# Time-step projection of the state-space branch: computed with the attention values, turned, and kept in DRAM

## The chip, the cores and the metric

The kernel runs on one core of one Trainium2 chip. Its time is the device time of one execution in microseconds (us); several executions are made and the median is given. Five engines work side by side, each with its own in-order queue of instructions: TensorE (PE in the profile, with its weight loads listed as PEld), VectorE (DVE), ScalarE (ACT), GpSimd (POOL) and SyncE (SP), which here only issues DMAs. Semaphores order the engines against each other. A profile is one execution recorded by the hardware; its clock starts with the first instruction, and its "span" is a little shorter than the device time of the same execution.

## The reference

One layer of a diffusion backbone over 512 latent tokens with 256 context tokens, model width 1024, float32. Cut to what matters here:

```python
p_lat = h_lat @ w_in                      # 512 x 1024 by 1024 x D_IN
p_ctx = h_ctx @ w_in                      # 256 tokens
# columns of w_in: z | x,B,C | dt (64) | q (1024) | k (256) | v (256) | gates
dt = softplus(p[..., DT0:Q0] + dt_bias)   # 2 directions x 32 heads
la = dt * (-exp(a_log))                   # log decay of each step
...                                       # chunked scans need cumulative sums of la
v_l = p_lat[..., V0:G0]                   # 4 value heads of 64
att = window_ctx_attention(q, k, v, kc, vc, sink)
out = (g_ssd * (y_ssd @ w_o_ssd) + g_att * (att @ w_o_att)) @ w_out
```

The 64 `dt` columns are the steps of the state-space branch. In the columns of `w_in` they lie apart from the 256 value columns, and nothing of the attention needs them; the state-space branch needs them before its first chunk.

## The kernel before

Every product is made in split float32: an operand x is rounded to a fast format (`hi`) and the rest x - hi is kept (`lo`), and three matmuls hi*hi, hi*lo, lo*hi are summed in PSUM. `load` (L154) fetches a weight piece of at most 128x1024 into one of three `wraw` buffers by a DMA on SP's queue, ACT rounds it to `whi` (L149), DVE subtracts to `wlo` (L150); there are two buffers each of `whi` and `wlo`. `run` (L167) loads one piece ahead of the step that uses it. The building tool then orders each engine's queue itself, by readiness and its own estimates, except where the code fixes PE's order.

The normal product `gemm` (L186) holds a 128x128 block of the weight matrix in the array and streams tokens: 512 latent columns, or 256 context columns, per matmul. Its output has channels on the partitions and tokens along the free axis. The values are made the other way round: `v_step` (L616) holds a 128-token block of the activations `hlh`/`hll` (latent) or `hch`/`hcl` (context) in the array and streams the 256 value columns of the weights, so that tokens come out on the partitions, as the attention's last product wants them. Six token blocks share three PSUM banks, two blocks of 256 columns to a bank. ACT and DVE then write `vst` as hi and lo (L633, L634).

The order of the work: modulation and norms; key, query and value steps; attention in 16 blocks (4 value heads by 4 query blocks, `block`, L650), between which query, key and `z` gate steps are set as other work for PE; then `att_split` (L834), three more `z` steps, and the attention's output projection in eight steps `oa_step` (L839). Behind the first of these stands `dt_tables` (L753): it makes the 64 `dt` columns with `gemm` (24 matmuls of 512 and 24 of 256 columns, 64 output channels, its own weight piece `wdt` of 128x512), adds the bias (L761, L762) and then works through softplus, logarithms, running sums and exponentials on ACT and DVE (L764 to L814), with small DMAs that park results in DRAM. The remaining `oa` steps keep PE at work meanwhile. `dt_turn` (L819) turns the tables by transposes on PE when the last `oa` step is through, and the state-space stage begins.

PSUM has eight banks. Up to `v_step` they are split as three `acc` and five `mis`; for the attention they are given to other pools (`psum_pools`, L648), and a new pool's bank is used once the old user of that bank has been read out.

Of the kernel before, what the change touches and what calls it, by code (L numbers as in the profile page):

```python
# [9 lines left out]
F32 = mybir.dt.float32  # L10
F32R = mybir.dt.float32r
U8 = mybir.dt.uint8
AF = mybir.ActivationFunctionType
ALU = mybir.AluOpType
# [4 lines left out]
P = 128  # L19
D = 1024  # L20
L = 512
LC = 256
KT = D // P
# [16 lines left out]
def raw(ap):  # L40
    return ap.bitcast(F32)
# [3 lines left out]
def tile_hybrid_layer(  # L45
# [11 lines left out]
    wk: bass.AP,  # L57
    wv: bass.AP,
    wq: bass.AP,
    wdt: bass.AP,  # L60
    wx: bass.AP,
    wz: bass.AP,
    wg: bass.AP,
# [13 lines left out]
    nc = tc.nc  # L77
    V, S, G, T = nc.vector, nc.scalar, nc.gpsimd, nc.tensor
# [5 lines left out]
    dpool = ctx.enter_context(tc.tile_pool(name="dpool", bufs=1, space=DRAM))  # L84
# [22 lines left out]
    def accb():  # L107
        return bank("acc")

    def misb():  # L110
        return bank("mis")
# [5 lines left out]


    src = {}
    src["dt", 0] = wdt, 512  # L120
    for i in range(2):
        src["k", i] = wk[i], 1024
        src["v", i] = wv[i], 1024
    for i in range(8):
        src["q", i] = wq[i], 1024
        src["oa", i] = woa[i], 1024
# [40 lines left out]
    def run(prog, ahead=1):  # L167
        seq = [k for keys, _ in prog for k in keys]
        have, nload, nuse = {}, 0, 0
        for keys, fn in prog:  # L170
            nuse += len(keys)
            while nload < min(nuse + ahead, len(seq)):
                have[seq[nload]] = load(seq[nload])
                nload += 1
            fn(*[have.pop(k) for k in keys])
# [10 lines left out]
    def gemm(targets, w, nk=KT, m=P, k0=0, first=True, last=True, ks=None):  # L186
        hi, lo = w
        for k in range(nk) if ks is None else ks:
            wh, wl = hi[:, k * m : (k + 1) * m], lo[:, k * m : (k + 1) * m]
            a, b = first and k == 0, last and k == nk - 1  # L190
            for ps, xh, xl in targets:
                T.matmul(ps, wh, xh[:, k0 + k, :], start=a, stop=False)  # L192
                T.matmul(ps, wh, xl[:, k0 + k, :], start=False, stop=False)  # L193
            for ps, xh, xl in targets:
                T.matmul(ps, wl, xh[:, k0 + k, :], start=False, stop=b)  # L195
            if BETWEEN and k % 3 == 1:
                BETWEEN.pop(0)()
# [21 lines left out]
    ao_d = dpool.tile([8, P, L], F32, name="ao_d")  # L219
    yz_d = dpool.tile([16, P, L], F32, name="yz_d")  # L220
    cs_d = dpool.tile([64, L], F32, name="cs_d")
    tt_d = dpool.tile([64, 4], F32, name="tt_d")

    def col(base, i):
# [72 lines left out]
    with tc.tile_pool(name="spool", bufs=1) as sp:  # L297
# [206 lines left out]
        for i in range(NG):  # L504
            t = tmp("tb")
# [109 lines left out]

    def v_step(*w):  # L616

        pos = [misb() for _ in range(3)]
        for k in range(KT):
            wh, wl = (z[:, (k % 4) * 256 : (k % 4 + 1) * 256] for z in w[k // 4])  # L620
            for p, po in enumerate(pos):
                hh, hl, c0 = (hlh, hll, 2 * p) if p < 2 else (hch, hcl, 0)
                for t in range(2):
                    c = slice((c0 + t) * P, (c0 + t + 1) * P)
                    o = po[:, t * 256 : (t + 1) * 256]
                    T.matmul(o, hh[:, k, c], wh, start=k == 0 and t == 0, stop=False, skip_group_check=True)
                    T.matmul(o, hh[:, k, c], wl, start=False, stop=False, skip_group_check=True)
                    T.matmul(o, hl[:, k, c], wh, start=False, stop=k == KT - 1, skip_group_check=True)
        for p, po in enumerate(pos):
            for t in range(2):  # L630
                o = po[:, t * 256 : (t + 1) * 256].rearrange("p (h d) -> p h d", h=4)
                v = vst[:, 2 * p + t, :, :]
                S.copy(v[:, :, 0:64], o)  # L633
                V.tensor_tensor(v[:, :, 64:128], o, raw(v[:, :, 0:64]), ALU.subtract)  # L634

    def q_step(t):
        def fn(w):
            ps = accb()
            gemm([LAT(ps)], w)
            q_split(ps, t)  # L640

        return [("q", t)], fn

    k_step(0)[1](first["w"][0])
    q_step(0)[1](first["w"][1])
    run([q_step(1), ([("v", 0), ("v", 1)], v_step)])

    psum_pools(acc=(2, 1), score=(1, 2), pt=(3, 1), po=(1, 1))  # L648

# [100 lines left out]
    atth = ep.tile([P, 8, L], F32R, name="atth")  # L750
    attl = ep.tile([P, 8, L], F32R, name="attl")

    def dt_tables(w):  # L753
        pl, pc = accb(), accb()
        gemm([(pl[:64, :L], hlh, hll), (pc[:64, :LC], hch, hcl)], w, m=64)
        shp = [64, 768]
        v = ep.tile(shp, F32, tag="d0", name="dv")
        e = ep.tile(shp, F32, tag="d1", name="de")
        u = ep.tile(shp, F32, tag="d2", name="du")
        u2 = ep.tile(shp, F32, tag="d3", name="du2")  # L760
        S.activation(v[:, :L], pl[:64, :L], AF.Identity, bias=dtv[:, 0:1])  # L761
        S.activation(v[:, L:], pc[:64, :LC], AF.Identity, bias=dtv[:, 0:1])  # L762
        nA = cpool.tile([64, 1], F32, name="nA")
        S.activation(nA, dtv[:, 1:2], AF.Exp)  # L764
        V.tensor_scalar_mul(nA, nA, -1.0)
# [81 lines left out]
        return [("oa", o)], fn  # L847

    oas = [oa_step(o) for o in range(8)]
    run([([], att_split)] + fill[n1:n2] + oas[:1] + [([("dt", 0)], dt_tables)] + oas[1:] + [([], dt_turn)])  # L850
    epool.close()
    att_pool.close()

# [588 lines left out]
def pack(  # L1442
# [31 lines left out]
    d["wm2"] = ca(w_mod[:, 2048:].reshape(4, 2, P, 8, 512).transpose(3, 0, 2, 1, 4).reshape(8, 4, P, 1024))  # L1474
    d["wq"] = _cols(w_in, perm(q0, 16))
    d["wk"] = _cols(w_in, perm(k0, 4))
    d["wv"] = ca(w_in[:, v0:g0].reshape(2, 4, P, 256).transpose(0, 2, 1, 3).reshape(2, P, 1024))
    d["w0"] = ca(w_in[:, g0 : g0 + 640].reshape(KT, P, 640))
    d["wdt"] = ca(w_in[:, dt0:q0].reshape(KT, P, 64).transpose(1, 0, 2).reshape(P, 512))
    d["wx"] = _cols(w_in, A(xbc0, dt0))  # L1480
    d["wz"] = _cols(w_in, A(z0, xbc0))
    d["wg"] = _cols(w_in, A(g0, g0 + 2048))
# [30 lines left out]
```

## Time and profile before

| | |
|---|---|
| median of 3 runs | 1293.3 us (1292.84 to 1293.32) |
| the profiled execution, its own time | 1291.25 us |
| its span | 1289.5 us |
| PE busy | 1260.1 us, 98% of the span |
| DVE / ACT / POOL busy | 899.2 / 664.8 / 138.6 us |
| DMA | 168.66 MB, mean 131 GB/s |

A line of the timeline reads: start, duration, engine, line of the code, operation, output<-inputs, shape, count, and in brackets how long the engine sat idle before it and which engine's work released it. The recorded duration of a matmul contains its way through the array, and the next one starts before it ends; what a matmul costs in a stream is the distance from its start to the next start. A row of stretches ("windows") gives, for a stretch of the span, the busy time of PE, PEld, DVE, ACT and POOL with the number of instructions in brackets, then the granted TensorE clock, the share of DMA and GB/s. A row of groups gives line, engine, operation, shape, count, busy time, mean of one in ns, and idle time ahead. A row of waits gives who waited for whom: us in total, how often, the longest.

### The profile page before, as it was taken

To read this page: it belongs to the slowest core of one execution; us is meant where nothing else is said; L and a number is where in the kernel's file an instruction comes from. 1 tells how busy PE (TensorE), PEld (TensorE's weight loads), DVE (VectorE), ACT (ScalarE), POOL (GpSimd) and SP (SyncE) were. 2 spreads that over 40 slices of the span, in tenths; PEclk is the share of its full clock that TensorE was granted. 3 is DMA by queue.
4 is the path that set the end of the run, shared out by engine and by line. 5 is a ranking of instruction groups with operands and counts; after the bars stand their busy time and mean duration, and the time that the engine had idled before them with its cause. 6 is when DMAs were issued, how large, how long until landed. Compare 5 with 4: busy or idle time off the path is not lost.

```text
span 1289.5 us, 17298 instructions
## 1 busy us (share of the span) xinstructions
PE 1260.1 (98%) x6482; PEld 1025.6 (80%) x6482; DVE 899.2 (70%) x1431; ACT 664.8 (52%) x1230; POOL 138.6 (11%) x113
## 2 busy tenths in 40 slices
PE   7999999999999999999999999999999999999997
PEld 4698777887778878788787777888888888888886
DVE  3867888778495588888888757776677767772323
ACT  3568888767434466475673744223544444442221
POOL 0000000000000043433434440000200000000000
PEclk9999999999999999999999999999999999999999
DMA  8621112222345245454445558867133433333331
GB/s 321 255 94 51 42 58 66 66 74 66 99 127 184 82 117 137 139 134 131 137 140 170 165 192 290 252 221 229 33 115 115 131 114 114 115 107 93 92 101 66
DMA packets 86931, 168.66 MB, mean 131 GB/s; under 512 B 6784, under 2 KB 42112, under 8 KB 86848
## 3 DMA queue, kind: packets, MB, share of 16 engines
q1 hardware_dynamic: 86848, 167.56, 41.5%
q8 instruction: 51, 0.84, 0.3%
q14 instruction: 32, 0.26, 0.1%
HBM read 150.62 MB, written 16.91 MB: 130 GB/s over the span
## 4 chain that ended last, share of the span: by engine, by line
PE 84%; DVE 7%; ACT 5%; issue 2%; DMA 1%; POOL 0%; SPq 0%; DVEq 0%; ACTq 0%; POOLq 0%
PE acc L193 21%; PE acc L192 21%; PE acc L195 21%; PE mis L1054 2%; PE mis L1047 2%; PE score L668 2%; PE pt L697 2%; PE mis L404 2%; PE mis L960 1%; PE po L702 1%; DVE wlo L150 1%; PE mis L888 1%; PE mis L978 1%; PE po L703 1%; PE acc L1196 1%
## 5 line engine op out<-in xcount | busy, mean ns | idle before, releaser
L150 DVE TENSOR_TENSOR wlo<-wraw,whi 128x1024 fp32r<-128x1024 f32 x161 | 203.8, 1266 | 133.0 <-ACT whi L149 131.7
L149 ACT CAST whi<-wraw 128x1024 fp32r<-128x1024 f32 x161 | 166.7, 1036 | 220.7 <-PE acc L193 186.6
L192 PE MATMUL acc<-hlh,whi 128*128 128x512 f32 (+1 forms) x496 | 204.1, 412 | 0.1
L193 PE MATMUL acc<-hll,whi 128*128 128x512 f32 (+1 forms) x496 | 196.1, 395 | 0.0
L195 PE MATMUL acc<-hlh,wlo 128*128 128x512 f32 (+1 forms) x496 | 195.4, 394 | 0.2 <-DVE wlo L150 0.2
L192 PE MATMUL acc<-mh,whi 128*128 128x512 f32 x376 | 146.5, 390 | 0.0
L193 PE MATMUL acc<-ml,whi 128*128 128x512 f32 x376 | 146.4, 389 | 0.0
L195 PE MATMUL acc<-mh,wlo 128*128 128x512 f32 x376 | 146.3, 389 | 0.0
L192 PEld LDWEIGHTS acc<-hlh,whi 128*128 128x128 f32 (+1 forms) x496 | 93.0, 187 | 21.3 <-issue 4.1
L193 PEld LDWEIGHTS acc<-hll,whi 128*128 128x128 f32 (+1 forms) x496 | 93.0, 187 | 19.9 <-issue 4.1
L195 PEld LDWEIGHTS acc<-hlh,wlo 128*128 128x128 f32 (+1 forms) x496 | 92.8, 187 | 19.5 <-issue 1.0
L195 PEld LDWEIGHTS acc<-mh,wlo 128*128 128x128 f32 x376 | 70.6, 188 | 14.8
L192 PEld LDWEIGHTS acc<-mh,whi 128*128 128x128 f32 x376 | 70.6, 188 | 14.7
L193 PEld LDWEIGHTS acc<-ml,whi 128*128 128x128 f32 x376 | 70.6, 188 | 14.6 <-DVE ml L1165 0.2
L962 POOL TENSOR_TENSOR st<-st,eT 128x512 f32<-128x512 f32 x24 | 32.8, 1368 | 410.3 <-ACT st L980 396.7
L860 ACT ACTIVATE ta<-acc,half 128x512 f32<-128x512 f32 (+1 forms) x66 | 46.6, 706 | 41.0 <-PE acc L195 41.0
L245 POOL TENSOR_TENSOR rs<-ms,phalf 128x2 f32<-128x2 f32 (+1 forms) x7 | 6.1, 877 | 548.9 <-DVE ms L244 548.9
L675 DVE CUSTOM_DVE_ANT_0 p<-score,winm,nsink 128x512 f32<-128x512 f32 (+1 forms) x64 | 52.0, 812 | 15.0 <-PE score L668 14.2
L192 PE MATMUL acc<-fh,whi 128*128 128x512 f32 x154 | 60.0, 390 | 0.0
L195 PE MATMUL acc<-fh,wlo 128*128 128x512 f32 x154 | 59.9, 389 | 0.0
L193 PE MATMUL acc<-fl,whi 128*128 128x512 f32 x154 | 59.9, 389 | 0.0
L679 ACT ACTIVATE p<-p,mneg 128x512 f32<-128x512 f32 (+1 forms) x64 | 49.7, 777 | 17.2 <-DVE mneg L675 16.9
(320 smaller groups left out, 2818.8 us busy)
## 6 DMA issues: line engine op xcount, KB each, us to landing
wraw<-wup SPq DMA_DIRECT2D x44, 512.0 KB, 3.6
fb<-cs_d SPq DMA_DIRECT2D x32, 512.0 KB, 6.7
wraw<-wm SPq DMA_DIRECT2D x32, 512.0 KB, 3.6
wraw<-wx SPq DMA_DIRECT2D x24, 512.0 KB, 3.6
wm<-wm SPq DMA_DIRECT2D x16, 512.0 KB, 8.1
wraw<-wz SPq DMA_DIRECT2D x16, 512.0 KB, 3.6
wraw<-wos SPq DMA_DIRECT2D x16, 512.0 KB, 4.6
wraw<-wdn SPq DMA_DIRECT2D x16, 512.0 KB, 3.5
```

The source lines that it names most:

```text
L149: S.copy(hi[:, :n], r[:, :n])
L150: V.tensor_tensor(lo[:, :n], r[:, :n], raw(hi[:, :n]), ALU.subtract)
L192: T.matmul(ps, wh, xh[:, k0 + k, :], start=a, stop=False)
L193: T.matmul(ps, wh, xl[:, k0 + k, :], start=False, stop=False)
L195: T.matmul(ps, wl, xh[:, k0 + k, :], start=False, stop=b)
L404: T.matmul(pg[i], w[a][:, i * P : (i + 1) * P], h[b], start=st and a + b == 0, stop=en and a == 1, skip_group_check=True,)
L668: T.matmul(ps[:, o : o + w], Q[h][:, b * P : (b + 1) * P], k[:, j, z[0] * P : z[0] * P + w], start=v == 0 and o % 512 in (0, P), stop=v == ...
L675: V.tensor_tensor_reduce(p[:, :n], ps[:, o0 : o0 + n], m, op0=ALU.add, op1=ALU.min, scale=1.0, scalar=nsink[:, h : h + 1], accum_out=mn,)
L679: S.activation(p[:, :n], p[:, :n], AF.Exp, bias=mn, scale=-1.0, accum_out=den[:, i : i + 1])
L697: T.transpose(pt[:, i * P : (i + 1) * P], pts[i][:, c * P : (c + 1) * P], ident)
L860: S.activation(o[:, :n], ps[:, :n], AF.Identity, scale=hcol(base_w, stride + i), bias=hcol(base_b, i))
L962: G.tensor_tensor(h8(n), h8(s), bc64(eT[:, z0 : z0 + 8, c]), ALU.mult)
```

## The change

The 64 step columns are joined to the 256 value columns on the host: the weight array `wv` becomes three pieces of 960, 960 and 640 columns (three, three and two blocks of 128 input rows with 320 columns each), and `wdt` goes. `v_step` now streams 320 columns per matmul, with each of the six token blocks in a PSUM bank of its own (five `mis`, one `acc`); the number of matmuls stays 144. After each block's two `vst` operations ACT copies the 64 step columns to SBUF (`steps`), PE turns the six 128x64 blocks by transposes into two banks, ACT copies these out, and two DMAs on SP's queue write them to a new DRAM array `dt_d` (64x768). `dt_tables` has no product any more: it reads `dt_d` by one DMA on SP's queue into `v` and adds the bias there in one ACT instruction.

```diff
     src = {}
-    src["dt", 0] = wdt, 512
+    for i, n in enumerate((3, 3, 2)):
+        src["v", i] = wv[i, :, : n * 320], n * 320
     for i in range(2):
         src["k", i] = wk[i], 1024
-        src["v", i] = wv[i], 1024
...
+    dt_d = dpool.tile([64, L + LC], F32, name="dt_d")
...
     def v_step(*w):
 
-        pos = [misb() for _ in range(3)]
+        pos = [misb() for _ in range(5)] + [accb()]
         for k in range(KT):
-            wh, wl = (z[:, (k % 4) * 256 : (k % 4 + 1) * 256] for z in w[k // 4])
-            for p, po in enumerate(pos):
-                hh, hl, c0 = (hlh, hll, 2 * p) if p < 2 else (hch, hcl, 0)
-                for t in range(2):
-                    c = slice((c0 + t) * P, (c0 + t + 1) * P)
-                    o = po[:, t * 256 : (t + 1) * 256]
-                    T.matmul(o, hh[:, k, c], wh, start=k == 0 and t == 0, stop=False, skip_group_check=True)
-                    T.matmul(o, hh[:, k, c], wl, start=False, stop=False, skip_group_check=True)
-                    T.matmul(o, hl[:, k, c], wh, start=False, stop=k == KT - 1, skip_group_check=True)
-        for p, po in enumerate(pos):
-            for t in range(2):
-                o = po[:, t * 256 : (t + 1) * 256].rearrange("p (h d) -> p h d", h=4)
-                v = vst[:, 2 * p + t, :, :]
-                S.copy(v[:, :, 0:64], o)
-                V.tensor_tensor(v[:, :, 64:128], o, raw(v[:, :, 0:64]), ALU.subtract)
+            wh, wl = (z[:, (k % 3) * 320 : (k % 3 + 1) * 320] for z in w[k // 3])
+            for t, po in enumerate(pos):
+                hh, hl, c0 = (hlh, hll, t) if t < 4 else (hch, hcl, t - 4)
+                c, o = slice(c0 * P, (c0 + 1) * P), po[:, 0:320]
+                T.matmul(o, hh[:, k, c], wh, start=k == 0, stop=False)
+                T.matmul(o, hh[:, k, c], wl, start=False, stop=False)
+                T.matmul(o, hl[:, k, c], wh, start=False, stop=k == KT - 1)
+        steps = tmp("te")
+        for t, po in enumerate(pos):
+            o = po[:, 0:256].rearrange("p (h d) -> p h d", h=4)
+            S.copy(vst[:, t, :, 0:64], o)
+            V.tensor_tensor(vst[:, t, :, 64:128], o, raw(vst[:, t, :, 0:64]), ALU.subtract)
+            S.copy(steps[:, t * 64 : (t + 1) * 64], po[:, 256:320])
+        for t0, t1 in ((0, 4), (4, 6)):
+            ps, n = misb(), (t1 - t0) * P
+            for t in range(t0, t1):
+                T.transpose(ps[:64, (t - t0) * P : (t - t0 + 1) * P], steps[:, t * 64 : (t + 1) * 64], ident)
+            o = tmp("tc")
+            S.copy(o[:64, :n], ps[:64, :n])
+            nc.sync.dma_start(dt_d[:, t0 * P : t1 * P], o[:64, :n])
...
-    run([q_step(1), ([("v", 0), ("v", 1)], v_step)])
+    run([q_step(1), ([("v", i) for i in range(3)], v_step)])
...
-    def dt_tables(w):
-        pl, pc = accb(), accb()
-        gemm([(pl[:64, :L], hlh, hll), (pc[:64, :LC], hch, hcl)], w, m=64)
+    def dt_tables():
         shp = [64, 768]
         v = ep.tile(shp, F32, tag="d0", name="dv")
...
-        S.activation(v[:, :L], pl[:64, :L], AF.Identity, bias=dtv[:, 0:1])
-        S.activation(v[:, L:], pc[:64, :LC], AF.Identity, bias=dtv[:, 0:1])
+        nc.sync.dma_start(v, dt_d)
+        S.activation(v, v, AF.Identity, bias=dtv[:, 0:1])
...
-    run([([], att_split)] + fill[n1:n2] + oas[:1] + [([("dt", 0)], dt_tables)] + oas[1:] + [([], dt_turn)])
+    run([([], att_split)] + fill[n1:n2] + oas[:1] + [([], dt_tables)] + oas[1:] + [([], dt_turn)])
```

More of the change, by code (lines that the diff above doesn't have):

```diff
@@ L59, in tile_hybrid_layer @@
     wq: bass.AP,
-    wdt: bass.AP,
     wx: bass.AP,
@@ L1476, in pack @@
     d["wk"] = _cols(w_in, perm(k0, 4))
-    d["wv"] = ca(w_in[:, v0:g0].reshape(2, 4, P, 256).transpose(0, 2, 1, 3).reshape(2, P, 1024))
+    vdt = ca(w_in[:, np.r_[v0:g0, dt0:q0]].reshape(KT, P, 320).transpose(1, 0, 2)).reshape(P, KT * 320)
+    d["wv"] = ca(np.pad(vdt, ((0, 0), (0, 320))).reshape(P, 3, 960).transpose(1, 0, 2))
     d["w0"] = ca(w_in[:, g0 : g0 + 640].reshape(KT, P, 640))
-    d["wdt"] = ca(w_in[:, dt0:q0].reshape(KT, P, 64).transpose(1, 0, 2).reshape(P, 512))
     d["wx"] = _cols(w_in, A(xbc0, dt0))
```

## The prediction

> **What bounds the kernel now.** I read the page first (busy shares, clock, chain), then the stretches and waits of the attention, then the timeline where the change takes something away or puts something in.
>
> ```profile
> span 1289.5 us, 17298 instructions
> PE 1260.1 (98%) x6482; PEld 1025.6 (80%) x6482; DVE 899.2 (70%) x1431; ACT 664.8 (52%) x1230; POOL 138.6 (11%) x113
> ...
> PEclk9999999999999999999999999999999999999999
> ...
> PE 84%; DVE 7%; ACT 5%; issue 2%; DMA 1%; POOL 0%; SPq 0%; DVEq 0%; ACTq 0%; POOLq 0%
> ```
>
> PE is busy throughout at full clock, and 84% of the chain that ended last is PE. So a matmul taken out is worth its distance to the next start, and anything that makes PE stand still costs its full length. Only the attention comes near another limit:
>
> ```profile
> 0.00:10.00 10.00, 3.18 (x20) 1.36 (x20) 1.22 (x8) 1.87 (x3) 0.74 (x9) 1.00 0.78 268
> ...
> 110.00:162.00 52.00, 50.90 (x280) 40.83 (x278) 46.59 (x100) 47.06 (x95) 0.00 (x0) 1.00 0.13 41
> 200.00:314.00 114.00, 113.72 (x609) 92.11 (x608) 89.79 (x191) 85.59 (x169) 0.00 (x0) 1.00 0.22 69
> ```
> ```profile
> PE pt L697 <- ACT p L688: 1.2, 1, 1.2
> PE po L702 <- ACT pth L700: 0.7, 2, 0.5
> ```
>
> From 110 to 162 us DVE (46.59) and ACT (47.06 of 52) are at 90%; from 200 on they have room. The longest wait of PE between 98.5 and 330 us is 1.2.
>
> **The product that goes.** The step columns are made between these two starts:
>
> ```profile
> 343.61 0.40 PE L192 MATMUL acc<-hlh,whi 128*64 128x512 f32 x1
> ...
> 351.90 0.40 PE L192 MATMUL acc<-atth,whi 128*128 128x512 f32 x1
> ```
>
> 351.90 - 343.61 = 8.3 us of PE without a gap: -8.3. Its split goes too, but the three new value pieces (960, 960, 640) hold as many columns as the two old ones and the step piece, so ACT and DVE have the same to round.
>
> **The wider value product.** The 144 matmuls stay and stream 320 columns instead of 256.
>
> ```profile
> 81.11 0.28 PE L626 MATMUL mis<-whi,hlh 128*128 128x256 f32 x1
> ...
> 98.29 0.28 PE L627 MATMUL mis<-wlo,hch 128*128 128x256 f32 x1
> 98.41 0.28 PE L628 MATMUL mis<-whi,hcl 128*128 128x256 f32 x1
> 98.53 0.40 PE L192 MATMUL acc<-hlh,whi 128*128 128x512 f32 x1
> ...
> 101.28 0.39 PE L192 MATMUL acc<-hlh,whi 128*128 128x512 f32 x1
> 101.51 0.39 PE L193 MATMUL acc<-hll,whi 128*128 128x512 f32 x1
> ```
>
> A start every 0.120 us at 256 columns, 0.23 at 512; on the line between them 320 columns take 0.1475. 144 x 0.0275 = +4.0, bounds 3.8 and 4.2. The second weight piece is now needed after three blocks of input rows instead of four. Its `wlo` is made here:
>
> ```profile
> 88.64 1.22 DVE L150 TENSOR_TENSOR wlo<-wraw,whi 128x1024 fp32r<-128x1024 f32 x1
> ...
> 89.96 0.34 PE L627 MATMUL mis<-wlo,hlh 128*128 128x256 f32 x1
> ```
>
> Before, PE reached it at 89.96, just as it was ready. Now it arrives at 81.11 + 54 x 0.1475 + the same 0.1 of start-up = 89.2, plus one matmul, while DVE, whose order there is the same, ends near 89.8: +0.5 (0 if DVE comes earlier, 0.7 at most). The third piece has until the sixth block: no cost.
>
> **The turn.** In the order in which the new kernel is built the six transposes stand directly behind the last value product, so PE, in order, stands until ACT has brought out all six step blocks. Before, 15 query matmuls followed there and hid ACT's copies.
>
> ```profile
> 98.01 1.37 ACT L633 CAST vst<-mis 128x256 fp32r<-128x256 f32 x4 [0.29 <-PE mis L628]
> 99.27 1.06 ACT L149 CAST whi<-wraw 128x1024 fp32r<-128x1024 f32 x1
> ...
> 98.42 1.48 DVE L634 TENSOR_TENSOR vst<-mis,vst 128x256 fp32r<-128x256 f32 x4 [0.24 <-ACT vst L633]
> ...
> 391.74 0.60 PE L827 MATMUL mis<-ident,dsb 128*128 128x128 f32 x4
> 392.27 0.33 PE L831 MATMUL mis<-ident,dsa 64*128 64x64 f32 x2
> ```
> ```profile
> L832 ACT COPY TC<-mis 128x128 f32<-128x128 f32 x1 | 0.3, 290 | 0.0
> ```
>
> Call T the moment PE could issue on. The last value matmul's record ends 0.16 after it (98.41 + 0.28 against 98.53); in the last round a block is done every 3 x 0.1475 = 0.44, so block 0 is ready at T - 2.05. ACT then has six `vst` copies (1.37/4 = 0.34), six step copies (estimate 0.25, under the 0.29 of a 128x128 copy) and, in its new order between the fourth and fifth of them, one `whi` rounding of 1.05: 2.0 + 1.5 + 1.05 = 4.6, so T + 2.55. Each step copy also waits for DVE's subtraction of its block (0.37 each, beside it): +0.2. Only the last transpose (0.13) is left then: PE goes on at T + 2.9. Ends: 1.9 if the rounding falls behind the copies, 3.7 if a step copy takes a `vst` copy's time and waits grow; I take +2.9. The turn uses the banks of blocks 0 and 1, and one of them goes to the score pool; its copy out (about 0.6 on ACT, ended by T + 3.4) is through when PE, after three query matmuls (0.7), comes to the first score at T + 3.6: 0, and up to 0.6 if the copies are late. The two writes to `dt_d` stand on SP's queue behind the four weight loads that PE needs next and ahead of two whose buffers are not free yet: 0, covered by the loads' own wait; the one value load more is paid for by the step load that goes.
>
> **The tables.** The chain of `dt_tables` starts behind `att_split` instead of behind the product, some three steps earlier. On ACT and DVE it now lies across the `z` steps:
>
> ```profile
> 329.09 1.05 ACT L149 CAST whi<-wraw 128x1024 fp32r<-128x1024 f32 x1
> 332.70 1.05 ACT L149 CAST whi<-wraw 128x1024 fp32r<-128x1024 f32 x1 [2.55 <-PE acc L193]
> ...
> 354.65 0.85 ACT L767 ACTIVATE de<-de 64x768 f32<-64x768 f32 x1
> ...
> 355.53 0.55 DVE L768 TENSOR_SCALAR du<-de 64x768 f32<-64x768 f32 x1 [1.15 <-ACT de L767]
> 356.12 4.95 DVE L769 RECIPROCAL du<-du 64x768 f32<-64x768 f32 x1
> ...
> 338.17 0.39 PE L192 MATMUL acc<-atth,whi 128*128 128x512 f32 x1
> ...
> 384.83 0.39 PE L193 MATMUL acc<-attl,whi 128*128 128x512 f32 x1
> 386.18 0.50 PE L195 MATMUL acc<-atth,wlo 128*128 128x512 f32 x1 [0.96 <-DVE wlo L150]
> ```
>
> On the old clock, and in the built order of the new kernel, ACT comes to the bias after the rounding that ends at 330.1, three instructions of 0.85 end at 332.65, DVE adds (0.55) and takes the reciprocal to 338.15. Behind it in DVE's new order stand the `z` read-out (0.6) and then the `wlo` of the first output step (1.2): ready at 339.9. PE starts that step at 338.17 and wants `wlo` two matmuls later, 338.62: +1.3 (0 if the chain is late enough to let the split ahead, 2 at most). The later splits lead their use by 3 us or more, but the one behind the running sums just arrives. The old stall at 384.83 (1.35 from start to start instead of 0.23: 1.1) goes with the chain's earlier end: -1.1. The read of `dt_d` waits on SP for PE, at the latest for the attention's last product:
>
> ```profile
> 323.35 0.43 PE L703 MATMUL po<-ptl,vst 128*128 128x512 f32 x1
> ```
> ```profile
> fb<-cs_d SPq DMA_DIRECT2D x32, 512.0 KB, 6.7
> ...
> ts_d<-tb SPq DMA_DIRECT2D x8, 256.0 KB, 2.1
> ```
>
> From 323.8 it lands after 2.1 to 6.7, at 325.9 to 330.5; ACT wants it at 330.1. I take 0 (the 192 KB lie nearer the 256 KB row), at most 0.4. [...]
>
> **The sum** on the profiled execution: -8.3 + 4.0 + 0.5 + 2.9 + 1.3 - 1.1 = -0.7. Then the attention, whose first score was here:
>
> ```profile
> 101.96 0.28 PE L668 MATMUL score<-khi,q 128*128 128x256 f32 x1
> ```
>
> It moves to 98.5 + 4.0 + 0.5 + 3.6 = 106.6, 4.6 later, while PE is 7.4 behind (4.0 + 0.5 + 2.9): only 3 query matmuls stand ahead of the first score in the built order, where 15 stood, so 12 x 0.227 = 2.7 us of covering work move into the stretch where ACT and DVE are at 90%. What they fill there is regained, 0 to 2.7; PE's recorded idle time from 110 to 162 is 52 - 50.9 = 1.1, starts lie late also without idle time, so I take the half, -1.3. In all -2.0: 1289.2 for the execution that took 1291.25. That execution lies 2.05 under the median of 1293.3; taken off the median: 1291.3. About 0.2%, 2.6 us, is what a measurement of this kernel can tell from no change, and -2.0 lies inside.
>
> **Rivals.** *The attention is bound by ACT and DVE (faster).* For it: the 90%. Against: PE hardly idles. All 2.7 come back and the first output step's split slips ahead of the reciprocal: -0.7 - 2.7 - 1.3 = -4.7, 1288.6.
>
> *The transposes of the attention lose their cover (slower).* In the new order of PE the first block's transposes stand 26 projection matmuls behind the first score instead of 32, the fourth block's 93 instead of 105. If softmax is not ready sooner, PE stands for what is missing, 18 x 0.227 = 4.1, and nothing is regained: -0.7 + 4.1 = +3.4, 1296.7. It decides once PE waits 3.3 us more than now at L697 and L702. Against: most other blocks have more cover than before.
>
> *The clock falls at the turn.* The turn makes the longest stand of PE inside the kernel's body. If PE ran at half its rate afterwards for as long as it stood, 2.9 us, half of that is lost: -2.0 + 1.5 = -0.5, 1292.8. Against it: in the first 10 us PE was busy for 3.18 only and the granted clock is 1.00 all the same. [...]
>
> **How the numbers follow.** Forecast as summed, its regained part between nothing and most of the 2.7: chance 0.60, of which 0.20 is faster by over 2.6. ACT and DVE as the bound: 0.20, faster. Lost cover: 0.16, slower. Clock: 0.04, half of it slower. So faster 0.40, same 0.42, slower 0.18. The forecast's own range is 1289.5 to 1292.6; with the rivals 8 in 10 lie between 1287.5 and 1295.5.
>
> **What would show it.** The value matmuls 0.1475 apart; PE standing some 2 to 3 us at the six transposes; a wait of about 1.3 for `wlo` in the first output step and none near the running sums; no 64-channel products behind the first output step. I am wrong if the turn costs 1 or 5, or if PE's waits inside the attention change by more than 3.

## The result, and the profile after

The changed kernel takes 1296.16 us (median of 7 executions, 1293.60 to 1299.63), the kernel before, run beside it on the same chip, 1292.84 (7 executions, 1291.53 to 1293.32). The ratio is 1.0029, with a 95% interval of 1.0015 to 1.0043: slower by 0.3%. Forecast was 1291.3, between 1289.5 and 1292.6; with the rivals the range ended at 1295.5, and the result lies above that too. The profiled execution of the changed kernel took 1295.57 us with a span of 1293.8; that of the kernel before 1291.25 and 1289.5. So the traces are 4.3 us apart, the medians 3.3. In the changed kernel the lines from L191 on are one lower than before in `gemm` (L194 is the product with `wlo`), and four to five higher in the attention (L673 is the score, L680 the row maximum, L702 the transposes, L707 and L708 the last products).

Where the 4.3 us come in is read from the starts of the same instructions in both timelines:

| on PE | before | after | later by |
|---|---|---|---|
| first value product | 81.11 | 81.53 | 0.42 |
| last value product | 98.41 | 102.50 | 4.09 |
| first query product behind the value step and the turn | 98.53 | 104.61 | 6.08 |
| first score | 101.96 | 105.39 | 3.43 |
| first output step | 338.17 | 348.87 | 10.70 |
| turn of the tables | 391.31 | 393.54 | 2.23 |
| first down step | 1156.40 | 1160.21 | 3.81 |
| end of the span | 1289.5 | 1293.8 | 4.3 |

From 98.53 to 338.17 the kernel before needs 239.64 us; the changed one needs 244.26 from 104.61 to 348.87: 4.6 more for the same 1243 matmuls. From the first output step to the turn of the tables it saves 8.47. The first view is the value step and the turn, on PE and then on ACT:

```profile
81.53 0.31 PE L624 MATMUL mis<-whi,hlh 128*128 128x320 f32 x1
...
102.50 0.31 PE L626 MATMUL acc<-whi,hcl 128*128 128x320 f32 x1
102.65 1.04 PE L636 MATMUL mis<-ident,te 128*64 128x128 f32 x4
104.44 0.41 PE L636 MATMUL mis<-ident,te 128*64 128x128 f32 x2 [0.76 <-ACT te L632]
104.61 0.48 PE L191 MATMUL acc<-hlh,whi 128*128 128x512 f32 x1
```
```profile
103.12 0.22 ACT L632 COPY te<-mis 128x64 f32<-128x64 f32 x1
103.22 1.06 ACT L148 CAST whi<-wraw 128x1024 fp32r<-128x1024 f32 x1
104.17 0.22 ACT L632 COPY te<-mis 128x64 f32<-128x64 f32 x1
104.27 0.23 ACT L632 COPY te<-acc 128x64 f32<-128x64 f32 x1
```

The value products start 20.97/143 = 0.147 us apart. The turn takes PE from 102.65 to 104.61, 1.96 us, with the weight rounding between the step copies. The second view is DVE's timeline around 155 us, then PE's; the third is PE's waits between 98 and 345 us.

```profile
149.97 0.75 DVE L680 CUSTOM_DVE_ANT_0 p<-score,winm,nsink 128x512 f32<-128x512 f32 x1
...
152.02 2.84 DVE L590 TENSOR_TENSOR klo<-tb,khi 64x512 fp32r<-64x512 f32 x4
155.13 1.77 DVE L590 TENSOR_TENSOR klo<-tc,khi 64x256 fp32r<-64x256 f32 x4 [0.28 <-ACT khi L589]
156.94 0.75 DVE L680 CUSTOM_DVE_ANT_0 p<-score,winm,nsink 128x512 f32<-128x512 f32 x1
```
```profile
154.70 0.39 PE L192 MATMUL acc<-hll,whi 128*128 128x512 f32 x1
157.75 0.38 PE L673 MATMUL score<-khi,q 128*128 128x256 f32 x1 [2.66 <-DVE mneg L680]
...
159.48 0.63 PE L191 MATMUL acc<-hlh,whi 128*128 128x512 f32 x1
159.91 0.63 PE L192 MATMUL acc<-hll,whi 128*128 128x512 f32 x1
```
```profile
PE score L673 <- DVE mneg L680: 3.3, 2, 2.7
PE po L707 <- ACT pth L705: 1.6, 4, 0.5
PE pt L702 <- ACT p L693: 1.3, 2, 1.2
```

All eight rests of the second key step (`klo`, 2.84 + 1.77 us) stand in DVE's queue in one lump ahead of a row maximum. The score bank is free only when that maximum has read it, so PE stands 2.66 us, the longest wait of the whole attention; the longest before was 1.2. Behind it the matmuls of 512 columns start 0.43 apart where they start 0.23 apart elsewhere. In the kernel before the same rests were spread out: the four of 512 columns stood one by one between 140.43 and 145.80, and only the four of 256 columns stood together ahead of a row maximum:

```profile
140.43 0.68 DVE L590 TENSOR_TENSOR klo<-tb,khi 64x512 fp32r<-64x512 f32 x1
...
149.22 0.75 DVE L675 CUSTOM_DVE_ANT_0 p<-score,winm,nsink 128x512 f32<-128x512 f32 x1
...
149.90 1.77 DVE L590 TENSOR_TENSOR klo<-tc,khi 64x256 fp32r<-64x256 f32 x4
151.70 0.75 DVE L675 CUSTOM_DVE_ANT_0 p<-score,winm,nsink 128x512 f32<-128x512 f32 x1
```

The fourth view is a row of stretches of the changed kernel, each 3.41 us long (the columns are those explained above; the clock is the third number from the end):

```profile
151.19:154.60 3.41, 3.41 (x18) 2.87 (x18) 3.27 (x6) 3.29 (x6) 0.00 (x0) 1.00 0.00 0
154.60:158.01 3.41, 0.75 (x5) 0.33 (x4) 3.01 (x8) 3.29 (x9) 0.00 (x0) 1.00 0.00 0
158.01:161.42 3.41, 3.30 (x12) 2.62 (x12) 3.30 (x5) 1.59 (x5) 0.00 (x0) 0.50 0.40 115
...
772.41:775.82 3.41, 1.87 (x13) 1.61 (x11) 1.48 (x3) 1.18 (x3) 1.02 (x1) 1.00 0.93 298
775.82:779.23 3.41, 3.23 (x8) 2.29 (x8) 3.41 (x6) 3.41 (x6) 0.00 (x0) 0.50 0.93 322
```

The clock is exactly halved for one stretch of 3.41 us (a cell, below) after PE was busy for only 0.75 us of the stretch before, and again at 775.82. A third such stretch lies at 28.3 us. In work that PE bounds each costs half its length, 1.7 us (an estimate from the length and the halved rate). The one at 775.82, where DVE and ACT are busy throughout, cost less: PE's lag behind the kernel before is 3.0 us at the product ahead of it and 3.6 behind it. The profiled execution of the kernel before has none inside its body, which is part of the 4.3 us between the traces; by the mean clocks of their executions (0.991 to 0.996 after; 0.991 to 0.998 before, in the sessions below) both kernels have some in most executions, the changed one about one more.

The last view is the first output step, DVE and then PE:

```profile
344.05 4.94 DVE L772 RECIPROCAL du<-du 64x768 f32<-64x768 f32 x1
...
349.46 1.20 DVE L149 TENSOR_TENSOR wlo<-wraw,whi 128x1024 fp32r<-128x1024 f32 x1
```
```profile
348.87 0.39 PE L191 MATMUL acc<-atth,whi 128*128 128x512 f32 x1
...
350.72 0.50 PE L194 MATMUL acc<-atth,wlo 128*128 128x512 f32 x1
```

`wlo` waits behind the reciprocal and the `z` read-out, as foreseen. Between 348.87 and 350.72 lie four matmuls, 0.9 us of work in 1.85: the hold-up costs 0.9. The longest wait recorded for PE there is another, 0.46 at 349.94 for a weight rounding on ACT, but it lies inside the same stretch: the product with `wlo` could not start before DVE's subtraction ended at 350.66.

### The profile page after: what moved, and what is told of

Read it like the earlier page. It is cut to its first block, busy times and chain, and to the rows that moved or that the text cites. A ratio compares the mean times of both kernels' runs of the same rounds, so it can differ in the third digit from the quotient of the medians.

```text
span 1293.8 us, 17232 instructions
## 1 busy us (share of the span) xinstructions
PE 1258.9 (97%) x6440; PEld 1027.5 (79%) x6440; DVE 899.7 (70%) x1431; ACT 666.1 (51%) x1237; POOL 138.4 (11%) x113
## 4 chain that ended last, share of the span: by engine, by line
PE 82%; ACT 7%; DVE 5%; issue 2%; DMA 2%; POOL 0%; SPq 0%; DVEq 0%; ACTq 0%; POOLq 0%
PE acc L194 20%; PE acc L191 20%; PE acc L192 20%; PE score L673 2%; PE mis L1057 2%; PE mis L1050 2%; PE pt L702 2%; PE mis L404 2%; PE mis L963 1%; PE po L707 1%; DVE wlo L149 1%; ACT whi L148 1%; PE po L708 1%; ACT ta L577 1%; PE mis L981 1%
## 5 line engine op out<-in xcount | busy, mean ns | idle before, releaser
L149 DVE TENSOR_TENSOR wlo<-wraw,whi 128x1024 fp32r<-128x1024 f32 (+1 forms) x161 | 203.9, 1267 | 136.9 <-ACT whi L148 131.5
L148 ACT CAST whi<-wraw 128x1024 fp32r<-128x1024 f32 (+1 forms) x161 | 166.6, 1035 | 220.9 <-PE acc L192 163.8
L191 PE MATMUL acc<-hlh,whi 128*128 128x512 f32 x488 | 201.7, 413 | 0.0
L194 PE MATMUL acc<-hlh,wlo 128*128 128x512 f32 x488 | 193.1, 396 | 0.5 <-DVE wlo L149 0.3
L192 PE MATMUL acc<-hll,whi 128*128 128x512 f32 x488 | 193.3, 396 | 0.0
L191 PE MATMUL acc<-mh,whi 128*128 128x512 f32 x376 | 146.6, 390 | 0.0
L194 PE MATMUL acc<-mh,wlo 128*128 128x512 f32 x376 | 146.4, 389 | 0.0
L191 PEld LDWEIGHTS acc<-hlh,whi 128*128 128x128 f32 x488 | 92.1, 189 | 20.3 <-issue 4.1
L194 PEld LDWEIGHTS acc<-hlh,wlo 128*128 128x128 f32 x488 | 92.0, 189 | 20.2 <-DVE wlo L149 1.5
L192 PEld LDWEIGHTS acc<-hll,whi 128*128 128x128 f32 x488 | 92.1, 189 | 20.0 <-issue 4.1
L194 PEld LDWEIGHTS acc<-mh,wlo 128*128 128x128 f32 x376 | 70.6, 188 | 14.8
L191 PEld LDWEIGHTS acc<-mh,whi 128*128 128x128 f32 x376 | 70.6, 188 | 14.3
L680 DVE CUSTOM_DVE_ANT_0 p<-score,winm,nsink 128x512 f32<-128x512 f32 (+1 forms) x64 | 52.0, 813 | 16.9 <-PE score L673 15.2
L191 PE MATMUL acc<-fh,whi 128*128 128x512 f32 x154 | 60.1, 390 | 0.0
L194 PE MATMUL acc<-fh,wlo 128*128 128x512 f32 x154 | 60.0, 389 | 0.0
```

The lines of the kernel that those rows point to most:

```text
L148: S.copy(hi[:, :n], r[:, :n])
L149: V.tensor_tensor(lo[:, :n], r[:, :n], raw(hi[:, :n]), ALU.subtract)
L680: V.tensor_tensor_reduce(p[:, :n], ps[:, o0 : o0 + n], m, op0=ALU.add, op1=ALU.min, scale=1.0, scalar=nsink[:, h : h + 1], accum_out=mn,)
```

## The experiments

Theory one was formed from the two traces: what makes the difference is one wait of PE behind the eight key rests, and the halved clock that follows it. Its rivals were that the attention as a whole is short of DVE and ACT, that every order of the attention has waits of its own, and, for the clock, that a stand must have a certain length. Each row of the table compares with the kernel before in the same session and on the same chip; e8, the kernel with the stands, was executed once, in 1310.14 us. Where the expectations of e1 and e2 speak of 244.3 and 239.6 us "between the first score and the first output step", they mean the stretch from the first query product; from the first score it is 243.5 and 236.2.

| run | median us | before us | ratio (95%) |
|---|---|---|---|
| e1 changed, key rests on POOL | 1292.60 | 1293.61 | 0.9991 (0.9980 to 1.0001) |
| e2 before, key rests on POOL | 1301.04 | 1293.61 | 1.0054 (1.0039 to 1.0069) |
| e3 before, key step one block earlier | 1299.86 | 1293.61 | 1.0045 (1.0030 to 1.0059) |
| e4 before, no step product | 1286.04 | 1293.61 | 0.9935 (0.9919 to 0.9951) |
| e5 changed, turn late | 1295.83 | 1293.40 | 1.0018 (1.0009 to 1.0028) |
| e6 changed, no turn | 1295.32 | 1293.40 | 1.0013 (1.0004 to 1.0022) |
| e7 changed, turn late, rests on POOL | 1291.44 | 1293.40 | 0.9986 (0.9977 to 0.9994) |
| e9 changed, raw steps kept | 1301.55 | 1293.24 | 1.0065 (1.0053 to 1.0078) |
| e10 the same, rests on POOL | 1296.29 | 1293.24 | 1.0027 (1.0016 to 1.0038) |
| e11 changed, half of the rests on POOL | 1294.55 | 1293.24 | 1.0008 (0.9998 to 1.0017) |
| e12 e10 with an early read | 1290.71 | 1293.58 | 0.9978 (0.9969 to 0.9987) |

**The key rests on POOL (e1, e2).** The edit, the same in both kernels:

```diff
-    def split_k(r, t, lo, hi):
+    def split_k(r, t, lo, hi, E=V):
...
-            for b in (0, 64):
+            for b in (a, 64 - a):
                 S.copy(khi[b : b + 64, j, lo:hi], r[a : a + 64, :n])
-                V.tensor_tensor(klo[b : b + 64, j, lo:hi], r[a : a + 64, :n], raw(khi[b : b + 64, j, lo:hi]), ALU.subtract)
+                z = a if E is G else b
+                E.tensor_tensor(klo[b : b + 64, j, lo:hi], r[a : a + 64, :n], raw(khi[z : z + 64, j, lo:hi]), ALU.subtract)
...
-            split_k(rope(pl, -0.125), t, 0, L)
+            split_k(rope(pl, -0.125), t, 0, L, G if t else V)
...
-            split_k(rc, t, L, 768)
+            split_k(rc, t, L, 768, G if t else V)
```

> The changed kernel, with the eight key rests (klo) of the second key step made on POOL instead of DVE; everything computed stays. Theory one (a single wait: the eight rests stand in DVE's queue ahead of a row maximum, PE stands 2.7 us behind it, and the clock is then halved for 3.4 us, which costs 1.7): the wait at the score matmul near 158 us goes and with it the halved clock behind it, so about 1296.2 - 2.7 - 1.7 = 1291.8, between 1291 and 1293. Rival (the attention as a whole is short of DVE and ACT or of cover for its transposes): the wait comes back at other places, the attention keeps its 244.3 us between the first score and the first output step, and the time stays between 1295 and 1297.

Measured: 1292.60, within the range and 3.6 us below the changed kernel's median; by the two ratios it is 0.0038 of 1293, or 4.9. PE's waits of the profiled execution:

```profile
PE score L674 <- DVE mneg L681: 1.8, 4, 0.7
```

The wait of 2.7 is gone, no halved clock lies between 17 and 1283 us, and PE comes to the first output step at 344.83 where it came at 348.87. Theory one holds in place and, within a microsecond, in size. What stays is 1.0 us: from its first query product behind the turn, at 104.25, the stretch takes 240.6, where the kernel before has 239.6. A second loss of about 2 us lies behind the tables: this execution is 1.8 us ahead of the kernel before at the turn of the tables (389.52 against 391.31) and 0.2 behind it at the first down step (1156.56 against 1156.40), at full clock throughout. One new wait of PE for DVE there is 1.1 (L234); the rest was not followed up. With 3.7 for the value step and 2.0 for the turn, these two losses use up the 8.5 us that the output steps save in this trace.

> The control for it: the kernel before, with the same eight key rests on POOL; everything computed stays. Theory one: the kernel before has no such wait, so taking 4.6 us of work off DVE changes little: 1292.8, between 1292 and 1294, with 239.6 us between first score and first output step. Rival (DVE bounds the attention): the kernel before gains too, 1 to 4 us, 1289 to 1292.

Measured: 1301.04, which neither expected. PE's waits, from 98 to 420 us, name the place:

```profile
PE acc L192 <- DVE te L522: 3.7, 1, 3.7
PE acc L195 <- DVE wlo L150: 2.3, 2, 1.3
```

The new built order lets a `z` read-out on DVE come late near 320 us, and two cells of halved clock follow there (321 to 328 us). Freeing DVE of 4.6 us made this order worse, so the attention isn't simply short of DVE; and moving these rests to POOL is no gain in itself. As a control it is a weak one, since the move gave the kernel before another order too.

**The lump put into the kernel before (e3).**

```diff
-    with_ = {(0, 2): [k_step(1)]}
+    with_ = {}
...
+    with_.setdefault((0, 1), []).append(k_step(1))
```

> The kernel before, with the second key step put one attention block earlier, behind block 1 instead of 2. In the built order this puts the eight key rests in one lump ahead of a row maximum, as in the changed kernel; everything computed stays, and value and step products are as before. Theory one: the lump alone makes PE wait 2 to 3 us at a score matmul, and a halved clock of 3.4 us follows: 1292.8 + 4.4 = 1297.2, between 1295 and 1298. Rival (the lump is covered, the loss comes from elsewhere in the change): 1292.8, between 1292 and 1294.

Measured: 1299.86, beyond the upper end. The waits from 98 to 345 us:

```profile
PE pt L697 <- DVE p L690: 4.5, 2, 4.1
PE score L668 <- DVE mneg L675: 1.6, 1, 1.6
```

The lump does make PE wait at the score, but for 1.6, and no halved clock follows there. The larger loss is another wait that the new order has near 320 us, 4.1, with two half-clock cells behind it. So the lump is a cause, of 1.6 to 2.7 according to what else stands around it, and it isn't what made this kernel slow.

**The product alone (e4).**

```diff
-    def dt_tables(w):
-        pl, pc = accb(), accb()
-        gemm([(pl[:64, :L], hlh, hll), (pc[:64, :LC], hch, hcl)], w, m=64)
+    def dt_tables():
...
-        S.activation(v[:, :L], pl[:64, :L], AF.Identity, bias=dtv[:, 0:1])
-        S.activation(v[:, L:], pc[:64, :LC], AF.Identity, bias=dtv[:, 0:1])
+        nc.sync.dma_start(v, xT[0, 0:64, 0:768])
+        S.activation(v, v, AF.Identity, bias=dtv[:, 0:1])
```

> The kernel before without its product for the 64 step columns: the tables are made from a 64x768 piece of the input array, read by one DMA, so the product of the steps is left out and the rest is as before. Prediction's step: -8.3 for the product, +0.6 for a rounding rest that comes late in the first output step (measured in the changed kernel), -1.1 for the old stall near 385 us: 1292.8 - 8.8 = 1284.0, between 1283 and 1285.5. Rival (part of the product filled a wait that then shows): only -5 to -7, 1286 to 1288.

Measured: 1286.04, ratio 0.9935, which is -8.4 us (-6.3 to -10.5), and in the trace 8.41 less from the first output step to the turn of the tables; the attention is unchanged. That is the -8.3 with what comes and goes beside it. The median of 1286 lies a little above the range, on a chip where before stood at 1293.6.

**The turn moved or left out (e5, e6).** In e5 the two loops of transposes, copies and writes are a step of their own behind the first attention block; in e6 they and the step copies are gone.

```diff
+    def turn_steps():
+        steps = STEPS["t"]
+        for t0, t1 in ((0, 4), (4, 6)):
+            ps, n = bank("pt"), (t1 - t0) * P
...
+            if (j, b) == (0, 0):
+                main.append(([], turn_steps))
```

> The changed kernel, with the turn of the steps taken out of the value step and set behind the first attention block; the step copies stay where they are, everything computed stays. The built order has 18 query matmuls ahead of the first score again, and a row maximum stands between the first and the last four key rests of the second key step. Theory one (turn 1.96, wait behind the key rests 2.7, halved clock 1.7): the stand at the turn goes and the 2.7 us wait shrinks to under 1, so 1296.2 - 2.0 - 2.0 - 1.7 = 1290.5, between 1289 and 1292.5. Rival (every new order of the attention has its own waits, as in the two changed orders of the kernel before): PE waits 2 us or more at some other place of the attention, and the time is 1293 to 1298.

> The changed kernel without the turn: no step copies, transposes, copies out or writes; the tables are made from a 64x768 piece of the input array, so the steps computed with the values are left out of what follows. It measures the wider value product and the missing step product alone: against the kernel before +3.7 (value step, as measured in the changed kernel) - 8.4 (product, as measured) = -4.7, so 1293.0 - 4.7 = 1288.3, between 1287 and 1290 if the attention keeps its time. Rival (the order of the attention decides): waits of 2 us or more inside the attention, 1291 to 1295.

Measured: 1295.83 and 1295.32, in both far above the forecast. PE's waits in e5, then in e6:

```profile
PE score L679 <- DVE mneg L686: 4.0, 3, 1.7
```
```profile
PE score L663 <- DVE mneg L670: 3.2, 3, 1.7
PE pt L692 <- ACT p L683: 2.0, 5, 1.2
```

e5's time lies in the rival's range and e6's 0.3 above it, though no single wait reaches 2 us. The kernel before has 0.4 at the score. In these orders four key rests stand ahead of each of two row maxima, and PE stands 0.6 and then 1.7 us behind them (1.75 at 158.93 in e5, 1.74 at 158.81 in e6); e5 has another wait of 1.6 at the first block. In e5 a cell at half clock follows at 158.64; in e6 none does, and its stretch up to the first output step still takes 244.1. Without any turn the kernel is hardly faster: the 1.96 us of the turn were not what decided, the order that the building tool gives the attention was.

**Both together (e7).**

> The changed kernel with both edits: the turn behind the first attention block, and the eight key rests of the second key step on POOL; everything computed stays. If the two gains add (wait and clock 3.6 as measured with the rests on POOL, turn 2.0): 1296.2 - 3.6 - 2.0 = 1290.6, faster than both kernels. Rival (a new order brings a new wait, as with the rests on POOL in the kernel before): 1293 to 1298.

The edit is e5's with e1's. Measured: 1291.44, ratio 0.9986, faster than both. The score waits are 2.3 in all, the longest 1.6 and that at the first block, and no half-clock cell lies inside the body of the profiled execution.

**The clock (e8).** PE was made to stand at known places in an otherwise quiet stage:

```diff
+    STANDS, STOOD = (1, 1, 2, 2, 2, 3), []
...
+            with tc.manual_schedule(engines={mybir.EngineType.PE}):
+                if STOOD:
+                    T.transpose(misb()[:, :P], STOOD.pop()[:, :P], ident)
...
+            if o < 6:
+                x = tmp("ta")
+                for c in range(STANDS[o]):
+                    V.tensor_scalar(x, ps if c == 0 else x, 1.0, None, ALU.mult)
+                STOOD.append(x)
```

> The kernel before, with PE made to stand between the down steps at the end: a transpose that waits for a chain of one to three copies on DVE is put first in the next step's order, six times, about 1 us twice, 2.4 us three times and 4.4 us once (estimates from DVE's 0.69 to 0.75 us for 128x512); everything computed stays. Theory one (the clock is judged in a fixed grid of 3.41 us, and a cell in which PE is busy for less than about half is followed by a cell at half clock): none after the stands of 1 us, always after the one of 4.4, and after those of 2.4 only where most of the stand lies in one cell. Rival (a stand must last 3.4 us by itself): half clock after the one of 4.4 alone. Rival (every stand of over 2 us halves the clock): after all four.

The stands on PE came out shorter than estimated, two of 0.79 and these four:

```profile
1208.65 0.33 PE L1359 MATMUL mis<-ident,ta 128*128 128x128 f32 x1 [1.78 <-DVE ta L1365]
1225.83 0.30 PE L1359 MATMUL mis<-ident,ta 128*128 128x128 f32 x1 [1.87 <-DVE ta L1365]
1244.63 0.30 PE L1359 MATMUL mis<-ident,ta 128*128 128x128 f32 x1 [1.87 <-DVE ta L1365]
1263.25 0.30 PE L1359 MATMUL mis<-ident,ta 128*128 128x128 f32 x1 [3.34 <-DVE ta L1365]
```

The stretches below are cells of 3.41 us counted from the moment at which the trace first records the full clock:

```profile
1206.13:1209.54 3.41, 1.63 (x9) 1.04 (x8) 2.63 (x4) 1.68 (x2) 0.00 (x0) 1.00 0.40 137
1209.54:1212.95 3.41, 3.41 (x17) 2.81 (x16) 0.79 (x2) 0.00 (x0) 0.00 (x0) 1.00 0.52 154
1223.19:1226.60 3.41, 1.54 (x8) 1.02 (x7) 2.60 (x4) 1.68 (x2) 0.00 (x0) 1.00 0.42 144
1226.60:1230.02 3.42, 3.42 (x10) 2.66 (x9) 0.82 (x2) 0.00 (x0) 0.00 (x0) 0.50 0.49 152
1240.26:1243.67 3.41, 2.50 (x12) 1.73 (x10) 1.42 (x3) 1.05 (x1) 0.00 (x0) 1.00 0.49 151
1243.67:1247.08 3.41, 2.45 (x12) 2.07 (x13) 2.55 (x4) 0.63 (x1) 0.00 (x0) 1.00 0.19 23
1247.08:1250.49 3.41, 3.41 (x17) 2.83 (x16) 0.00 (x0) 0.24 (x1) 0.00 (x0) 1.00 0.33 133
1260.74:1264.15 3.41, 0.90 (x5) 0.80 (x6) 2.96 (x5) 1.06 (x3) 0.00 (x0) 1.00 0.28 47
1264.15:1267.56 3.41, 3.41 (x10) 2.64 (x9) 0.00 (x0) 0.00 (x0) 0.00 (x0) 0.50 0.35 131
```

Two stands of the same 1.87 us had opposite results: the one that lay within a cell (PE busy 1.54 of 3.41) was followed by a cell at half clock, the one that two cells shared (2.50 and 2.45) was not. So neither a length of 3.4 us nor a length of 2 told the stands apart; in this stage PE's busy time in the cell did: 1.54 and 0.90 us of 3.41 were followed by half clock, 1.63, 2.45 and 2.50 were not. The waits of e5 and e6 agree: the 1.75 left PE busy for 1.33 us of one cell, and half clock followed; the 1.74 was shared by two cells (2.05 and 2.01), and none did. The same instructions got other cells in another execution: up to 1171 us PE, DVE and ACT run the same instructions in the same order in e8 as in the kernel before, yet e8's trace has half-clock cells at 28.5 and 776.0 us and that of the kernel before has none there.

**Raw steps kept (e9, e10, e12).** To take the turn out of the attention altogether, the step copies go to DRAM untransposed and are turned at the tables, into the PSUM banks from which the kernel before added the bias:

```diff
-        nc.sync.dma_start(v, dt_d)
+        pl, pc, steps = accb(), accb(), tmp("te")
+        nc.sync.dma_start(steps[:, :384], dt_d)
+        for t in range(6):
+            T.transpose((pl, pc)[t // 4][:64, t % 4 * P : (t % 4 + 1) * P], steps[:, t * 64 : (t + 1) * 64], ident)
```

> The changed kernel without a turn in the value step: the step copies go to DRAM as they are (128x384) by one DMA, come back at the tables, and six transposes there bring them into PSUM, where the bias is added as in the kernel before; everything computed stays. The built order still has all eight key rests in one lump ahead of a row maximum. Theory one (the lump makes the wait, whatever stands at the turn): a wait of 2 to 3 us at a score matmul near 157 us and a halved clock behind it in most executions; 1296.2 - 2.0 for the turn + 0.8 for the transposes = 1295.0, between 1293.5 and 1296.5. Rival (the turn's 2 us shift everything and cause the wait): the wait goes too, 1290 to 1292.

> The same with the eight key rests of the second key step on POOL; everything computed stays. Theory one: the wait and the halved clock go, 3.6 less than with the lump: 1291.4, between 1290 and 1292.5, faster than the kernel before by about 0.1 to 0.2%. Rival (new waits of the new order): 1293 to 1297.

Measured: 1301.55 and 1296.29, 6.6 and 4.9 above what was expected (e10's lies in the rival's range). PE's waits in e9:

```profile
PE score L667 <- DVE mneg L674: 4.3, 2, 2.7
PE acc L756 <- DMA te<-dt_d: 4.0, 1, 4.0
```

The lump made its 2.7 here too, with the turn gone, so the turn's shift isn't the cause of that wait; and e10 without the lump is 5.3 faster than e9. Not all of that is the lump: in the traces the stretch up to the first output step is 2.5 shorter (242.1 against 244.6, and e10 has a half-clock cell near 326 us in it), while 3.45 lie behind the tables, where e9 has a half-clock cell at 780 us. What kept both slow was a new wait that the edit itself brought: the read of the steps stood on SP's queue behind the `z` steps' writes, went out at 353.2 (352.6 in e10) and left PE standing for 4.0 us, with a halved cell after it. The next run gave the read a buffer of its own and put it ahead of the last `z` write:

```diff
+    steps = ep.tile([P, 384], F32, name="dsteps")
+    nc.sync.dma_start(steps, dt_d)
+
     def dt_tables():
-        pl, pc, steps = accb(), accb(), tmp("te")
-        nc.sync.dma_start(steps[:, :384], dt_d)
+        pl, pc = accb(), accb()
```

> The kernel with raw steps in DRAM and the eight key rests on POOL, with the read of the steps put into a buffer of its own and ahead of the z steps' last writes on SP's queue, where the run before had it behind them; everything computed stays. Theory one: the wait of 4.0 us for that read and the halved clock behind it (1.7) go: 1296.3 - 5.7 = 1290.6, between 1289.5 and 1292, faster than both kernels. Rival (a wait removed comes back elsewhere): 1293 to 1296.

Measured: 1290.71, ratio 0.9978 (0.9969 to 0.9987). The read goes out at 328.1 and nobody waits for it. Against e10 the trace saves 4.7 from the first output step to the turn of the tables and 1.6 ahead of it, where e10's half-clock cell near 326 us is missing. This is the change in the form in which it pays: 0.2% faster than the kernel before, and 0.5% faster than the change as it was made.

**Half of the rests on POOL (e11).** The edit is e1's, with `G` for the four context rests alone.

> The changed kernel, with only the four context rests of the second key step (1.77 us on DVE) on POOL; the four latent ones (2.84 us) stay in DVE's order ahead of the row maximum; everything computed stays. Theory one: the wait of 2.7 shrinks by the 1.8 taken away, to about 0.9, too short for a halved clock: 1292.6 (all eight on POOL) + 0.9 = 1293.5, between 1292.5 and 1294.5. Rival (the first rests are what matters, or the wait has another cause): the wait stays above 2 and the time at 1295 to 1297.

Measured: 1294.55, just above the range. The longest score wait of the profiled execution is 0.7, where 0.9 was expected, and no halved clock follows; but its order has 1.0 us of waits for `wlo` where e1's has 0.3, and this dose is worth 1.6 by the medians, not the 2.7 expected.

## Why the prediction was wrong

**The product that goes: right.** -8.3 was forecast; with the hold-up in the first output step (+1.3 forecast, 0.9 measured) and the old stall near 385 us that goes (-1.1) the forecast for this stage was -8.1, and 8.47 were measured; e4 has 8.41. The read of `dt_d` held its 0 as described: the whole stage is 10.7 us later than on the old clock, and with that taken off the read went out at 323.8 and ACT came to the bias at 330.0, as assumed. It landed 3.1 us after its issue, between the two rows quoted.

**The wider value product: right.** +4.0 was forecast, 3.8 to 4.2; it is 20.97 - 17.30 = +3.7 from first to last start. The late `wlo` of the second piece, +0.5, did not come.

**The turn: mis-sized.** The mechanism is the one described, down to the rounding between the fourth and the fifth step copy; the cost is 1.96, near the lower end of 1.9, for 2.9. A step copy is recorded with 0.22, but the next ACT instruction starts 0.10 to 0.17 after it, so that a copy takes that much and not the 0.25 estimated; over six copies that is most of the 0.9.

**"The attention regains half of 2.7": this step failed.** -1.3 was forecast; the stretch became 4.6 longer. Nothing of the 12 query matmuls was regained: even with the rests on POOL 1.0 was lost. The step looked at PE's order and at the share of ACT and DVE, and took DVE's order inside the attention as given. But the order of every queue was built anew, and in the new one eight rests stood ahead of a row maximum: 2.7 us of standing and a half-clock cell behind it, of which the trace of e1 gives back 3.7. Runs e1, e9 and e10 show that; where the last 1.0 comes from stays open; e2, e3, e5 and e6 show that other orders lose as much at other places. The prediction's own condition for being wrong, PE's waits inside the attention changed by more than 3, is met: 6.7 without the turn, where they were 3.1.

**The rivals.** The transposes did not lose their cover: at L702 and L707 PE waits 3.1 us in all, where it waited 2.3 at L697 and L702, against the 3.3 more that were to decide. ACT and DVE as a bound that gives time back is refuted too. The clock, at 0.04, was the underrated one: not at the turn (PE busy for 2.65 of that cell's 3.41 us, no halving in this execution) but behind the longer wait, and for a whole cell of 3.41 us instead of for as long as PE stood.

**The evidence against the clock was misread.** The first 10 us were quoted with a clock of 1.00. The matmuls just behind them, in the kernel before, say otherwise:

```profile
13.78 1.05 PE L404 MATMUL mis<-ah,w0l 128*128 128x512 f32 x2
...
17.91 0.62 PE L404 MATMUL mis<-ah,w0l 128*128 128x512 f32 x2
```

Two matmuls of the same shape take 0.98 us up to the next one's start at 14.76, and 0.47 us (to 18.38) after 17.2 us, which is where the trace's records of the clock begin. So until about then the matmuls came at half the rate, and the 1.00 stood for a missing record. The traces give three more things: every halved stretch inside the changed kernel's body (at 28.30, 158.01 and 775.82) lasts 3.41 us; the cells do not start with the kernel (the first record lies at 17.2 us in the kernel before and at 14.9 in e8, whose instructions are the same there); and PE was not idle for a whole cell ahead of a halved one: 1.54 us of work in 3.41 (e8) was little enough.

What stays open: what the kernels lose behind the tables (1.6 us up to the first down step and 0.5 at the very end in the changed kernel's trace, only part of it by the cell at 775.82), and how many half-clock cells each kernel has on average; the mean clocks are too coarse to count them. Why a given order has its waits near 320 us (e2, e3) was not followed up.

## What to carry to other kernels

Where a tool sorts the queues, an edit ahead of a stage whose engines are 90% busy can be a new draw of that stage's order, as the edits ahead of the attention were here: compare the built order of each of its engines, and look for long groups ahead of the instruction that frees what PE needs next. Here a stand of PE cost its length, and up to 1.7 us more (the estimate above) where it left PE busy for 1.54 us or less of a 3.41 us cell (e8). A step that comes out early is worth its matmuls only if turning it, and reading it back, stand where nobody waits: e12 and the change differ by that and the rests alone, and by 5.5 us; the traces put 2.0 us of their difference behind the tables, in part the half-clock cell at 775.82.

## What the runs showed of the hardware

The granted clock of PE changed in cells of 3.41 us. In the traces of both kernels every change of it lies a whole number of cells behind the first record: in the changed kernel, with its first record at 14.65 us, the halved stretches begin 4, 42, 223 and 373 cells later, in the kernel before the only one 371 cells behind 17.20. Cells with PE busy for 0.75 us (changed kernel, 154.60), 0.90 (e8, 1260.74), 1.10 (e10, 352.98), 1.19 (changed kernel, 1284.41) and 1.54 (e8, 1223.19) were followed by one at half clock; those with 1.63 (e8, 1206.13) and 1.68 (e10, 349.57) were not. Above that the recorded busy time did not tell them apart: in the changed kernel 1.87 at 772.41 and 2.81 at 24.89 were, 1.84 at 1281.00 was not.

In e1 the key rests take 1.29 to 1.30 us on POOL at best, where DVE needs 0.69, and a weight rest on DVE that runs beside them takes 2.05 instead of 1.22:

```profile
151.47 6.24 POOL L591 TENSOR_TENSOR klo<-tb,khi 64x512 fp32r<-64x512 f32 x4 [93.80 <-ACT khi L589]
```
```profile
151.78 2.05 DVE L149 TENSOR_TENSOR wlo<-wraw,whi 128x1024 fp32r<-128x1024 f32 x1
```

Four rests take 6.24 us there, not 4 x 1.3 = 5.2: the weight rest lasts 0.83 longer, the slowest of the key rests (2.15) 0.85 longer than the median one. What held them up was not shown.
